# A hybrid decoder block on one core: every tile of its pool placed by hand

## The chip, the cores and the metric

The kernel runs on one core of one Trainium2 chip. The metric is device microseconds of one execution. Three runs of the kernel before took 1086.47, 1087.07 and 1087.11 us, so their median is 1087.07 us.

## The reference

One layer of a decoder, sequence 512, model width 1024, all in float32. It is cut here to what is computed.

```
h    = rms_norm(x)
proj = h @ w_in                    # glu | q | k | v | g | gate logits
a    = glu[..., :C] * sigmoid(glu[..., C:])
a    = silu(layer_norm(causal_depthwise_conv(a, 31 taps)))
y_a  = a @ w_conv_proj + b
r    = retention_chunkwise(rotary(q), rotary(k), v)   # 4 heads, dk 256, dv 512
y_b  = (silu(g) * head_norm(r)) @ w_ret_proj
x    = x + (sigmoid(gA) * y_a + sigmoid(gB) * y_b) @ w_out
u    = causal_depthwise_conv(rms_norm(x) @ w_up, 3 taps)
x    = x + (silu(u[..., :F]) * u[..., F:]) @ w_down   # F = 3072
out  = rms_norm(x)
```

## The kernel before

Activations are held transposed: 128 channels on the partitions, the 512 tokens along the row, so an activation tile is 128 x 512 in float32, 2048 bytes in each partition. Every activation that a matmul reads is split in two tiles of type float32r, a high and a low part, by ACT (a cast, L170 or L177) and DVE (a subtraction, L171 or L178). Weights come as one stream of 184 pieces of 128 x 1024 (4096 bytes in each partition, 8 blocks of 128 x 128): `load_half` (L93) loads a piece into `wraw`, `split_half` (L100) makes `whi` and `wlo` of it, again with ACT (L106) and DVE (L107). Each of the three tags has three buffers, and a piece is asked for two pieces ahead (`LOOK`).

Nearly all matmuls stand in `unit` (L143). For every block of weights there are three, each with 512 columns: the weight block is the stationary operand, which an own instruction (LDWEIGHTS) loads, the activation tile is the moving one.

```
wh, wl = blocks(1)
nc.tensor.matmul(ps, lhsT=wh, rhs=xh, start=kt == 0, stop=False)   # L147
nc.tensor.matmul(ps, lhsT=wh, rhs=xl, start=False, stop=False)     # L148
nc.tensor.matmul(ps, lhsT=wl, rhs=xh, start=False, stop=kt == last) # L149
```

Which tag the moving tile has depends on the stage:

- Four heads, one after the other: the gated convolution's, q's, k's and g's units move `xg` (the input). `values` (L421) is the other way round: `xg` is stationary and `whi` or `wlo` moves (L426 to L428). `ret_proj` of the head before moves `R`. `scores` (L452) has `A` on both sides, with 512, 384, 256 and 128 columns (L458 to L462); `inner` (L472) moves `sh` and `sl` against stationary `A` (L483 to L485).
- Gates and the last head's projection move `xg` and `R` in turns. The convolution's projection moves `A` (high) and `C` (low). The output projection moves `xg` (the mix).
- The up-projection moves `A`. The down-projection runs in two halves, the first over `xg` and `R`, the second over `C` and `xg`; its last two units are cut into halves of 256 tokens (L635 to L637).
- Sums over channels and their spread (L238, L191, L222) are a few dozen matmuls with `onesr`, `ones` and `identr`.

All tiles come from one pool, `sb`. A tag's buffers are laid out one behind another when the tag's first tile is asked for, so the order in which the program first asks for tags sets every address. Before, that order is the order of first use: `par` (2112 bytes) comes first, then `ones`, `neghalf` and so on as the code needs them. The same code lines set the order of the work: the scheduler orders instructions by the place where they are written and by `tc.high_priority`.

```
def t512(tag, bufs, dt=F32):                                        # L69
    return sb.tile([P, S], dt, tag=tag, bufs=bufs, name=nm(tag))
raw = sb.tile([P, HS], F32, tag="wraw", bufs=3, name=nm("wraw"))    # L94, whi and wlo alike
```

Of the kernel before, what the change touches and what calls it, by code (L numbers as in the profile page):

```python
# [9 lines left out]
F32 = mybir.dt.float32  # L10
F32R = mybir.dt.float32r
# [3 lines left out]
P = 128  # L15
S = 512
D = 1024
KT = D // P
# [3 lines left out]
NCH = S // P  # L22
# [3 lines left out]
FK = 3  # L26
EPS = 1e-6
HS = 8 * P
LOOK = 2
WARM = 9  # L30
WPRIO = 100
# [16 lines left out]
def hybrid_block(  # L48
# [11 lines left out]
    sb = ctx.enter_context(tc.tile_pool(name="sb", bufs=1))  # L60
# [4 lines left out]
    def nm(s):  # L65
        uid[0] += 1
        return f"{s}_{uid[0]}"

    def t512(tag, bufs, dt=F32):  # L69
        return sb.tile([P, S], dt, tag=tag, bufs=bufs, name=nm(tag))  # L70

    def tmp():
        return t512("t", 8)

    def bank():
        return psp.tile([P, S], F32, tag="ps", name=nm("ps"))

    def f32(ap):
        return ap.bitcast(F32)

    par = sb.tile([P, NPARAM], F32, tag="par", name="par")

    def pcol(name, i):
        c = _PC[name] + i
        return par[:, c:c + 1]
# [5 lines left out]
    raws = {}  # L91

    def load_half(h):  # L93
        raw = sb.tile([P, HS], F32, tag="wraw", bufs=3, name=nm("wraw"))  # L94
        cut = (0, 2 * P, HS) if h == 0 else (0, HS)
        raws[h] = raw, [slice(u, v) for u, v in zip(cut, cut[1:])]
        for sl in raws[h][1]:
            nc.sync.dma_start(out=raw[:, sl], in_=wst[h][:, sl])

    def split_half(h):  # L100
        raw, sls = raws.pop(h)
        hi = sb.tile([P, HS], F32R, tag="whi", bufs=3, name=nm("whi"))
        lo = sb.tile([P, HS], F32R, tag="wlo", bufs=3, name=nm("wlo"))
        with tc.high_priority(offset=WPRIO if h > 1 else 0):
            for sl in sls:
                nc.scalar.copy(out=hi[:, sl], in_=raw[:, sl])  # L106
                nc.vector.tensor_tensor(out=lo[:, sl], in0=raw[:, sl], in1=f32(hi[:, sl]),  # L107
                                        op=ALU.subtract)
        halves[h] = (hi, lo)

    def upto(h):
        while emitted[0] <= min(h, NBLK - 1):
            load_half(emitted[0])
            split_half(emitted[0])
            emitted[0] += 1
# [3 lines left out]
    def blocks(n):  # L119
        b = pos[0]  # L120
        pos[0] += n
        h, c = divmod(b, 8)
        upto(h + LOOK)
        hi, lo = halves[h]
# [18 lines left out]
    def unit(ps, rhs):  # L143
        last = len(rhs) - 1
        for kt, (xh, xl) in enumerate(rhs):
# [4 lines that stand above are left out]
        tick()  # L150
        return ps
# [15 lines left out]
    def split(src, tag, bufs):  # L167
        h = t512(tag, bufs, F32R)
        l = t512(tag, bufs, F32R)
        nc.scalar.copy(out=h, in_=src)  # L170
        nc.vector.tensor_tensor(out=l, in0=src, in1=f32(h), op=ALU.subtract)  # L171
        return h, l
# [21 lines left out]
    def tok(dt=F32):  # L194
        if dt == F32R:
            return sb.tile([P, NCH], F32R, tag="tokr", bufs=4, name=nm("tokr"))
        return sb.tile([P, NCH], F32, tag="tok", bufs=8, name=nm("tok"))
# [73 lines left out]
        later(wait[0], second)  # L271


    ones = sb.tile([P, P], F32, tag="ones", name="ones")
    nc.gpsimd.memset(ones, 1.0)
    neghalf = sb.tile([P, NCH], F32, tag="neghalf", name="neghalf")
    nc.gpsimd.memset(neghalf, -0.5)
    warm = tok()
    nc.scalar.copy(out=warm, in_=neghalf)
    warm_ps = bank()  # L280
    for _ in range(WARM):
        nc.tensor.matmul(warm_ps[:, 0:P], lhsT=ones, rhs=ones, start=True, stop=True)
    xs = []
    g0 = sb.tile([P, KT], F32, tag="g0", name="g0")
    for i in range(KT):
        t = t512("x", 8)
        nc.sync.dma_start(out=t, in_=xT[i * P:(i + 1) * P, :])
        xs.append(t)
        if i == 0:
            nc.sync.dma_start(out=g0, in_=params[:, _PC["norm_mix_g"]:_PC["norm_mix_g"] + KT])  # L290
            load_half(0)
        if i == 3:
            load_half(1)
    ident = sb.tile([P, P], F32, tag="ident", name="ident")
    nc.sync.dma_start(out=ident, in_=ident_in)
    nc.sync.dma_start(out=par, in_=params)
    identr = sb.tile([P, P], F32R, tag="identr", name="identr")
    nc.gpsimd.tensor_copy(out=identr, in_=ident)
    onesr = sb.tile([P, P], F32R, tag="onesr", name="onesr")
    nc.gpsimd.tensor_copy(out=onesr, in_=ones)  # L300
    xg = []
    for i in range(KT):
        xg.append(split_scaled(xs[i], g0[:, i:i + 1], "xg", 16))
        if i in (0, 3):
            split_half(emitted[0])
            emitted[0] += 1
# [13 lines left out]
    ss = SumSq()  # L320
    with tc.high_priority(offset=-200):
        for i in range(KT):
            ss.add(xs[i])
    r_tok = sb.tile([P, 4 * NCH], F32, tag="rtok", name="rtok")[:, 0:NCH]
    rB = [None]
    cosr = sb.tile([P, S], F32, tag="cosr", name="cosr")
    sinr = sb.tile([P, S], F32, tag="sinr", name="sinr")

    def norm_mix(b, ps):
        rB[0] = b  # L330
# [6 lines left out]
    def times_r(ps):  # L337
        t = tmp()
        nc.vector.tensor_tensor(out=t, in0=ps, in1=rB[0], op=ALU.mult)  # L339
        return t  # L340
# [106 lines left out]
    SOFF = (0, 512, 896, 1152)  # L447

    def scores(q, k, dec):
        sh = sb.tile([P, 1280], F32R, tag="sh", name=nm("sh"))  # L450
        sl_ = sb.tile([P, 1280], F32R, tag="sl", name=nm("sl"))
        for j in range(NCH):  # L452
            n = S - j * P
            ps = bank()
            js = slice(j * P, (j + 1) * P)
            for d in range(2):
                (qh, ql), (kh, kl) = q[d], k[d]
                nc.tensor.matmul(ps[:, :n], lhsT=kh[:, js], rhs=qh[:, j * P:], start=d == 0,  # L458
                                 stop=False)
                nc.tensor.matmul(ps[:, :n], lhsT=kh[:, js], rhs=ql[:, j * P:], start=False,  # L460
                                 stop=False)
                nc.tensor.matmul(ps[:, :n], lhsT=kl[:, js], rhs=qh[:, j * P:], start=False,  # L462
                                 stop=d == 1)
            t = tmp()
            nc.vector.tensor_tensor(out=t[:, :n], in0=ps[:, :n], in1=dec[:, :n], op=ALU.mult)
            o = slice(SOFF[j], SOFF[j] + n)
            nc.scalar.copy(out=sh[:, o], in_=t[:, :n])
            nc.vector.tensor_tensor(out=sl_[:, o], in0=t[:, :n], in1=f32(sh[:, o]),
                                    op=ALU.subtract)
        return sh, sl_  # L470
# [48 lines left out]
    for h in range(H):  # L519
        ps = [glu_units() for _ in range(2)] if h else glu_first()  # L520
        for i in range(2):
            a = glu(*ps[i])
            with tc.high_priority(offset=-1200):
                conv(2 * h + i, a)
        dec = t512("dec", 1)
        nc.sync.dma_start(out=dec, in_=decay[h])
        q = rope()
        k = rope()
        if rg is not None:
            ret_proj(h - 1, rg)  # L530
        v = values()
        sc = scores(q, k, dec)
        sgs = []
        for e in range(DV // P):
            t = times_r(unit(bank(), xg))
            s_ = t512("G", 4)
            nc.scalar.activation(out=s_, in_=t, func=AF.Silu)
            sgs.append(s_)
        banks = inner(sc, v)
        rg = ret_norm(h, banks, sgs)  # L540
# [16 lines left out]
    for m in range(KT):  # L557
        ps = unit(bank(), cv)
        t = tmp()
# [4 lines left out]
    ss = SumSq()  # L564
# [31 lines left out]
    def up_units():  # L596
        return unit(bank(), x1g), unit(bank(), x1g)
# [12 lines left out]
    first = [up_units() for _ in range(2)]  # L610
# [6 lines left out]
    ss = SumSq()  # L617
# [81 lines left out]
def _weight_stream(w_in, w_conv_proj, w_ret_proj, w_out, w_up, w_down):  # L699
# [14 lines left out]
    def rp(h):  # L714
        w = w_ret_proj[h * DV:(h + 1) * DV].reshape(4, P, KT // 2, 2, P)
        return w.transpose(2, 1, 3, 0, 4).reshape(KT // 2, P, HS)

    for h in range(H):
        for i in (2 * h, 2 * h + 1):
            pair = np.stack((wi[i], wi[KT + i]))  # L720
            if i == 0:
                pair = pair.reshape(2, P, KT, P).transpose(1, 2, 0, 3).reshape(P, 2, HS)
                pair = pair.transpose(1, 0, 2)
# [68 lines left out]
```

## Time and profile before

| | |
|---|---|
| median of three runs | 1087.07 us |
| the profiled execution | 1086.47 us |
| its span, first to last instruction | 1084.7 us |
| PE busy | 1073.2 us (99%) |
| PEld (weight loads, beside the matmuls) busy | 883.2 us (81%) |
| DVE busy | 770.0 us (71%) |
| ACT busy | 418.3 us (39%) |
| mean DMA rate over the span | 99 GB/s |

A busy time is the union of an engine's instructions. A matmul's row is longer than the distance to the next matmul, because the next one starts before the last one's results are out; so what one matmul costs in a stream is read from the starts of its rows, not from their durations. Line numbers here and in the rows are those of the kernel before.

### The profile page before, as it was taken

To read this page: it belongs to the slowest core of one execution; us is meant where nothing else is said; L and a number is where in the kernel's file an instruction comes from. 1 tells how busy PE (TensorE), PEld (TensorE's weight loads), DVE (VectorE), ACT (ScalarE), POOL (GpSimd) and SP (SyncE) were. 2 spreads that over 40 slices of the span, in tenths; PEclk is the share of its full clock that TensorE was granted. 3 is DMA by queue.
4 is the path that set the end of the run, shared out by engine and by line. 5 is a ranking of instruction groups with operands and counts; after the bars stand their busy time and mean duration, and the time that the engine had idled before them with its cause. 6 is when DMAs were issued, how large, how long until landed. Compare 5 with 4: busy or idle time off the path is not lost.

```text
span 1084.7 us, 12428 instructions
## 1 busy us (share of the span) xinstructions
PE 1073.2 (99%) x4834; PEld 883.2 (81%) x4834; DVE 770.0 (71%) x1126; ACT 418.3 (39%) x556; POOL 24.8 (2%) x88
## 2 busy tenths in 40 slices
PE   8999999999999999999999999999999999999996
PEld 6888888888888888888888888888888888888886
DVE  7899899758996699948764555677676236767433
ACT  6334332533234331535542234444443113444331
POOL 1000000000000000000000000000000000000000
PEclk9999999999999999999999999999999999999999
DMA  7223232323322232222323532332222223222212
GB/s 274 91 98 105 68 99 95 107 68 98 98 97 88 72 110 99 81 78 88 107 98 107 146 117 98 88 113 85 94 97 97 97 98 98 90 86 97 98 58 79
DMA packets 33259, 107.33 MB, mean 99 GB/s; under 512 B 3952, under 2 KB 6256, under 8 KB 33200
## 3 DMA queue, kind: packets, MB, share of 16 engines
q1 hardware_dynamic: 32416, 104.69, 29.1%
q0 software_dynamic: 784, 1.85, 1.0%
q8 instruction: 38, 0.62, 0.2%
q14 instruction: 21, 0.17, 0.1%
HBM read 104.41 MB, written 2.11 MB: 98 GB/s over the span
## 4 chain that ended last, share of the span: by engine, by line
PE 97%; issue 1%; DVE 1%; DMA 0%; SPq 0%; POOLq 0%; ACT 0%; POOL 0%; DVEq 0%
PE ps L147 28%; PE ps L149 28%; PE ps L148 28%; PE ps L427 3%; PE ps L426 3%; PE ps L428 3%; PE ps L484 1%; PE ps L485 1%; PE ps L483 1%; PE ps L460 0%; PE ps L462 0%; PE ps L458 0%; DVE ss L183 0%; DMA x<-in_xT_dram 0%; PE ps L238 0%
## 5 line engine op out<-in xcount | busy, mean ns | idle before, releaser
L106 ACT CAST whi<-wraw 128x1024 fp32r<-128x1024 f32 (+1 forms) x185 | 193.2, 1045 | 356.5 <-PE ps L148 258.3
L107 DVE TENSOR_TENSOR wlo<-wraw,whi 128x1024 fp32r<-128x1024 f32 (+1 forms) x185 | 224.7, 1215 | 62.1 <-ACT whi L106 61.9
L147 PE MATMUL ps<-xg,whi 128*128 128x512 f32 x672 | 262.1, 390 | 0.0
L148 PE MATMUL ps<-xg,whi 128*128 128x512 f32 x672 | 261.7, 389 | 0.0
L149 PE MATMUL ps<-xg,wlo 128*128 128x512 f32 x672 | 261.5, 389 | 0.0
L149 PE MATMUL ps<-A,wlo 128*128 128x512 f32 x448 | 176.5, 394 | 0.0
L147 PE MATMUL ps<-A,whi 128*128 128x512 f32 x448 | 176.5, 394 | 0.0
L368 DVE SCALAR_TENSOR_TENSOR C<-ap,par,C 128x512 f32<-128x512 f32 x240 | 166.4, 744 | 2.9 <-ACT C L365 2.6
L148 PE MATMUL ps<-A,whi 128*128 128x512 f32 x384 | 151.3, 394 | 0.0
L149 PEld LDWEIGHTS ps<-xg,wlo 128*128 128x128 f32 x672 | 126.2, 188 | 26.5
L147 PEld LDWEIGHTS ps<-xg,whi 128*128 128x128 f32 x672 | 126.2, 188 | 26.1
L148 PEld LDWEIGHTS ps<-xg,whi 128*128 128x128 f32 x672 | 126.2, 188 | 26.1
L149 PEld LDWEIGHTS ps<-A,wlo 128*128 128x128 f32 x448 | 83.8, 187 | 20.9
L147 PEld LDWEIGHTS ps<-A,whi 128*128 128x128 f32 x448 | 83.8, 187 | 20.7
L148 PEld LDWEIGHTS ps<-A,whi 128*128 128x128 f32 x384 | 71.8, 187 | 17.7
L589 DVE SCALAR_TENSOR_TENSOR t<-ap,par,t 128x512 f32<-128x512 f32 x96 | 71.7, 750 | 2.3 <-ACT t L586 0.7
L339 DVE TENSOR_TENSOR t<-ps,rB 128x512 f32<-128x512 f32 x48 | 32.5, 685 | 55.2 <-PE ps L149 55.2
L183 DVE TENSOR_TENSOR x<-x,ps 128x512 f32<-128x512 f32 (+1 forms) x50 | 33.0, 663 | 53.4 <-PE ps L149 49.9
L583 DVE TENSOR_TENSOR ap<-ps,rB 128x512 f32<-128x512 f32 x48 | 33.1, 691 | 48.4 <-PE ps L149 45.5
L147 PE MATMUL ps<-R,whi 128*128 128x512 f32 x160 | 63.0, 394 | 0.0
L148 PE MATMUL ps<-R,whi 128*128 128x512 f32 x160 | 63.0, 394 | 0.0
L149 PE MATMUL ps<-R,wlo 128*128 128x512 f32 x160 | 63.0, 394 | 0.0
(147 smaller groups left out, 1175.8 us busy)
## 6 DMA issues: line engine op xcount, KB each, us to landing
wraw<-in_wst_dram SPq DMA_DIRECT2D x183, 512.0 KB, 3.3
x<-in_xT_dram SPq DMA_DIRECT2D x16, 256.0 KB, 2.7
out_dram<-t SPq DMA_DIRECT2D x8, 256.0 KB, 2.3
nB<-row POOLq DMA_DIRECT2D x5, 256.0 KB, 4.7
dec<-in_decay_dram SPq DMA_DIRECT2D x4, 256.0 KB, 2.6
t<-in_cs_dram SPq DMA_DIRECT2D x2, 256.0 KB, 4.0
rB<-row POOLq DMA_DIRECT2D x2, 256.0 KB, 4.1
wraw<-in_wst_dram SPq DMA_DIRECT2D x1, 384.0 KB, 3.7
```

Source lines behind the costliest of these rows:

```text
L106: nc.scalar.copy(out=hi[:, sl], in_=raw[:, sl])
L107: nc.vector.tensor_tensor(out=lo[:, sl], in0=raw[:, sl], in1=f32(hi[:, sl]), op=ALU.subtract)
L147: nc.tensor.matmul(ps, lhsT=wh, rhs=xh, start=kt == 0, stop=False)
L148: nc.tensor.matmul(ps, lhsT=wh, rhs=xl, start=False, stop=False)
L149: nc.tensor.matmul(ps, lhsT=wl, rhs=xh, start=False, stop=kt == last)
L183: nc.vector.tensor_tensor(out=acc, in0=acc, in1=v, op=ALU.add)
L368: nc.vector.scalar_tensor_tensor(out=acc, in0=a[:, k:k + S], scalar=wcol(k), in1=acc, op0=ALU.mult, op1=ALU.add)
L426: nc.tensor.matmul(banks[c], lhsT=xh[:, sl], rhs=wh, start=kt == 0, stop=False)
L427: nc.tensor.matmul(banks[c], lhsT=xl[:, sl], rhs=wh, start=False, stop=False)
L428: nc.tensor.matmul(banks[c], lhsT=xh[:, sl], rhs=wl, start=False, stop=kt == KT - 1)
L583: nc.vector.tensor_tensor(out=u[:, FK - 1:], in0=ps, in1=rB[0], op=ALU.mult)
L589: nc.vector.scalar_tensor_tensor(out=c, in0=u[:, k:k + S], scalar=wcol(k), in1=c, op0=ALU.mult, op1=ALU.add)
```

## The change

No operation is added or taken away. All tiles of the pool but `junk`, `ap`, `vs`, `vm` and `tokr` are asked for at the top of the function, in an order written by hand; `first` keeps the first tile of each tag until the old place asks for it, through `t512` or the new helper `wide`. Small tiles stand first, then all tiles of 2048 bytes, then the weights' and the scores', and `par` behind them. The built programs hold the same instructions on every engine in the same order, with the same waits.

```
+    first = {}
     def t512(tag, bufs, dt=F32):
+        if tag in first:
+            t = first.pop(tag)
+            assert t.dtype == dt, tag
+            return t
         return sb.tile([P, S], dt, tag=tag, bufs=bufs, name=nm(tag))
...
+    ones = sb.tile([P, P], F32, tag="ones", name="ones")
+    ident = sb.tile([P, P], F32, tag="ident", name="ident")
+    identr = sb.tile([P, P], F32R, tag="identr", name="identr")
+    neghalf = sb.tile([P, NCH], F32, tag="neghalf", name="neghalf")
+    g0 = sb.tile([P, KT], F32, tag="g0", name="g0")
+    r_tok = sb.tile([P, 4 * NCH], F32, tag="rtok", name="rtok")[:, 0:NCH]
+    warm = sb.tile([P, NCH], F32, tag="tok", bufs=8, name="warm")
+    for tag, bufs, dt in (("x", 8, F32), ("xg", 16, F32R), ("A", 16, F32R), ("C", 8, F32),
+                          ("R", 8, F32R), ("G", 4, F32), ("ss", 2, F32), ("t", 8, F32),
+                          ("rB", 1, F32), ("nB", 1, F32), ("dec", 1, F32)):
+        first[tag] = sb.tile([P, S], dt, tag=tag, bufs=bufs, name=nm(tag))
+    cosr = sb.tile([P, S], F32, tag="cosr", name="cosr")
+    sinr = sb.tile([P, S], F32, tag="sinr", name="sinr")
+    for tag, dt in (("wraw", F32), ("whi", F32R), ("wlo", F32R)):
+        first[tag] = sb.tile([P, HS], dt, tag=tag, bufs=3, name=nm(tag))
+    for tag in ("sh", "sl"):
+        first[tag] = sb.tile([P, SW], F32R, tag=tag, name=nm(tag))
+    onesr = sb.tile([P, P], F32R, tag="onesr", name="onesr")
     par = sb.tile([P, NPARAM], F32, tag="par", name="par")
+
+    def wide(tag, dt, n, bufs):
+        if tag in first:
+            return first.pop(tag)
+        return sb.tile([P, n], dt, tag=tag, bufs=bufs, name=nm(tag))
...
-        raw = sb.tile([P, HS], F32, tag="wraw", bufs=3, name=nm("wraw"))
+        raw = wide("wraw", F32, HS, 3)
...
-        hi = sb.tile([P, HS], F32R, tag="whi", bufs=3, name=nm("whi"))
-        lo = sb.tile([P, HS], F32R, tag="wlo", bufs=3, name=nm("wlo"))
+        hi = wide("whi", F32R, HS, 3)
+        lo = wide("wlo", F32R, HS, 3)
...
-        sh = sb.tile([P, 1280], F32R, tag="sh", name=nm("sh"))
-        sl_ = sb.tile([P, 1280], F32R, tag="sl", name=nm("sl"))
+        sh = wide("sh", F32R, SW, 1)
+        sl_ = wide("sl", F32R, SW, 1)
```

The addresses that follow from the two orders, in bytes within a partition. "Over 512" and "over 2048" are the remainders of the first buffer's address; the buffers of a tag lie 2048 or 4096 bytes apart, so all of them have the same two.

| tag (buffers x bytes) | before | over 512 | over 2048 | after | over 512 | over 2048 |
|---|---|---|---|---|---|---|
| par (1 x 2112) | 16512 | 128 | 128 | 219648 | 0 | 512 |
| ones (1 x 512) | 18624 | 192 | 192 | 16512 | 128 | 128 |
| identr (1 x 512) | 48640 | 0 | 1536 | 17536 | 128 | 1152 |
| onesr (1 x 512) | 49152 | 0 | 0 | 219136 | 0 | 0 |
| x (8 x 2048) | 19456 | 0 | 1024 | 18432 | 0 | 0 |
| wraw (3 x 4096) | 35840 | 0 | 1024 | 172032 | 0 | 0 |
| xg (16 x 2048) | 49664 | 0 | 512 | 34816 | 0 | 0 |
| whi (3 x 4096) | 82432 | 0 | 512 | 184320 | 0 | 0 |
| wlo (3 x 4096) | 94720 | 0 | 512 | 196608 | 0 | 0 |
| t (8 x 2048) | 111104 | 0 | 512 | 145408 | 0 | 0 |
| C (8 x 2048) | 140736 | 448 | 1472 | 100352 | 0 | 0 |
| A (16 x 2048) | 159168 | 448 | 1472 | 67584 | 0 | 0 |
| sh (1 x 5120) | 192192 | 192 | 1728 | 208896 | 0 | 0 |
| sl (1 x 5120) | 197312 | 192 | 704 | 214016 | 0 | 1024 |
| R (8 x 2048) | 212672 | 192 | 1728 | 116736 | 0 | 0 |

## Rows read from the trace of the kernel before

**Rows 1.** The page: span, engines' busy time, chain that ended last.
```profile
span 1084.7 us, 12428 instructions
...
PE 1073.2 (99%) x4834; PEld 883.2 (81%) x4834; DVE 770.0 (71%) x1126; ACT 418.3 (39%) x556; POOL 24.8 (2%) x88
...
PE 97%; issue 1%; DVE 1%; DMA 0%; SPq 0%; POOLq 0%; ACT 0%; POOL 0%; DVEq 0%
```

**Rows 2.** Waits of PE, longest of 7: us in total, times, longest.
```profile
PE ps L222 <- DVE tokr L215: 1.2, 1, 1.2
```

**Rows 3.** Groups by line and form: xcount | busy us, mean ns.
```profile
L147 PE MATMUL ps<-xg,whi 128*128 128x512 f32 x672 | 262.1, 390 | 0.0
...
L147 PE MATMUL ps<-A,whi 128*128 128x512 f32 x448 | 176.5, 394 | 0.0
...
L148 PE MATMUL ps<-A,whi 128*128 128x512 f32 x384 | 151.3, 394 | 0.0
...
L147 PE MATMUL ps<-R,whi 128*128 128x512 f32 x160 | 63.0, 394 | 0.0
...
L148 PE MATMUL ps<-C,whi 128*128 128x512 f32 x88 | 34.7, 394 | 0.0
...
L147 PE MATMUL ps<-C,whi 128*128 128x512 f32 x24 | 9.5, 394 | 0.0
```

**Rows 4.** Timeline of PE, `xg` moving, first and last of 143: start us, us.
```profile
118.72 0.39 PE L147 MATMUL ps<-xg,whi 128*128 128x512 f32 x1
...
150.91 0.39 PE L148 MATMUL ps<-xg,whi 128*128 128x512 f32 x1
```

**Rows 5.** Timeline of PE: 96 rows of `values`, six of `scores` at 512 columns.
```profile
52.30 0.39 PE L426 MATMUL ps<-whi,xg 128*128 128x512 f32 x1
...
74.06 0.39 PE L458 MATMUL ps<-A,A 128*128 128x512 f32 x1
...
75.43 0.33 PE L458 MATMUL ps<-A,A 128*128 128x384 f32 x1
```

**Rows 6.** Timeline of PE: 96 rows of `R` in `ret_proj`, then `values`.
```profile
151.36 0.39 PE L147 MATMUL ps<-R,whi 128*128 128x512 f32 x1
...
173.76 0.39 PE L426 MATMUL ps<-whi,xg 128*128 128x512 f32 x1
...
174.91 0.39 PE L428 MATMUL ps<-wlo,xg 128*128 128x512 f32 x1
```

**Rows 7.** Timeline of PE, `A` moving in the up-projection: first, last of 169.
```profile
895.76 0.39 PE L147 MATMUL ps<-A,whi 128*128 128x512 f32 x1
...
934.96 0.39 PE L147 MATMUL ps<-A,whi 128*128 128x512 f32 x1
```

**Rows 8.** Timeline of PE at 256 columns: 12 rows of `C`, 24 of `xg`.
```profile
1055.92 0.28 PE L635 MATMUL ps<-C,whi 128*128 128x256 f32 x1
...
1057.33 0.28 PE L635 MATMUL ps<-xg,whi 128*128 128x256 f32 x1
...
1060.20 0.29 PE L635 MATMUL ps<-C,whi 128*128 128x256 f32 x1
```

**Rows 9.** Timeline of PE, first pass of `inner`: nine rows apart.
```profile
99.68 0.39 PE L483 MATMUL ps<-sh,A 128*128 128x512 f32 x1
...
101.27 0.22 PE L483 MATMUL ps<-sh,A 128*128 128x128 f32 x1
```

**Rows 10.** Groups by line and form, on DVE.
```profile
L171 DVE TENSOR_TENSOR xg<-t,xg 128x512 fp32r<-128x512 f32 x24 | 16.5, 688 | 10.3 <-ACT xg L170 10.3
...
L171 DVE TENSOR_TENSOR R<-G,R 128x512 fp32r<-128x512 f32 x16 | 10.9, 684 | 0.0
```

**Rows 11.** Three stretches: busy us of PE, PEld, DVE, ACT, POOL; clock, DMA.
```profile
151.00:174.00 23.00, 23.00 (x101) 18.44 (x100) 23.00 (x34) 9.21 (x14) 0.00 (x0) 1.00 0.31 99
440.00:528.00 88.00, 88.00 (x411) 74.06 (x410) 59.97 (x102) 40.60 (x59) 4.57 (x8) 1.00 0.28 88
894.00:1006.00 112.00, 112.00 (x482) 89.76 (x481) 77.01 (x96) 46.52 (x58) 1.72 (x17) 1.00 0.29 94
```

More of the change, by code (lines that the diff above doesn't have):

```diff
@@ L28 @@
 HS = 8 * P
+SW = 1280
 LOOK = 2
@@ L271, in stat @@
         later(wait[0], second)
-    ones = sb.tile([P, P], F32, tag="ones", name="ones")
     nc.gpsimd.memset(ones, 1.0)
-    neghalf = sb.tile([P, NCH], F32, tag="neghalf", name="neghalf")
     nc.gpsimd.memset(neghalf, -0.5)
-    warm = tok()
     nc.scalar.copy(out=warm, in_=neghalf)
@@ L283, in hybrid_block @@
     xs = []
-    g0 = sb.tile([P, KT], F32, tag="g0", name="g0")
     for i in range(KT):
@@ L293, in hybrid_block @@
             load_half(1)
-    ident = sb.tile([P, P], F32, tag="ident", name="ident")
     nc.sync.dma_start(out=ident, in_=ident_in)
     nc.sync.dma_start(out=par, in_=params)
-    identr = sb.tile([P, P], F32R, tag="identr", name="identr")
     nc.gpsimd.tensor_copy(out=identr, in_=ident)
-    onesr = sb.tile([P, P], F32R, tag="onesr", name="onesr")
     nc.gpsimd.tensor_copy(out=onesr, in_=ones)
@@ L323, in hybrid_block @@
             ss.add(xs[i])
-    r_tok = sb.tile([P, 4 * NCH], F32, tag="rtok", name="rtok")[:, 0:NCH]
     rB = [None]
-    cosr = sb.tile([P, S], F32, tag="cosr", name="cosr")
-    sinr = sb.tile([P, S], F32, tag="sinr", name="sinr")
     def norm_mix(b, ps):
```

## The prediction

> **What bounds the kernel now.** I read the page first: PE is busy for 1073.2 of 1084.7 us and holds 97% of the chain that ended last [rows 1]. Then the waits: the longest wait of PE for another engine is 1.2 us [rows 2], so between start and tail nothing but the matmul stream itself sets the time. The only question is how far apart two matmuls start, and whether that distance depends on an address.
>
> The groups by line give a first hint: matmuls of one shape last 390 ns with `xg` moving and 394 ns with `A`, `R` or `C` [rows 3]. Those durations overlap, so I took the distance of starts from the timeline:
>
> - `xg` moving: (150.91 - 118.72) / 142 = 226.7 ns [rows 4].
> - `whi` and `wlo` moving, `xg` stationary: (74.06 - 52.30) / 96 = 226.7 ns [rows 5].
> - `R` moving: (173.76 - 151.36) / 96 = 233.3 ns [rows 6].
> - `A` moving: (934.96 - 895.76) / 168 = 233.3 ns [rows 7].
>
> All have 512 columns, stationary blocks of the same size and the granted clock at 1.00, 2.4 GHz [rows 11]. `R` stands between stretches of `xg` and of `values`, with the same DVE load and DMA traffic around it, so the stage is not the cause. What the three tags at 233.3 share in the table of addresses: they start at a remainder of 448 or 192 over 512 bytes. What the others share: they start at a multiple of 512 (none at a multiple of 2048; all have 512 over 2048).
>
> **The change, part by part.** No instruction, wait or queue entry is added, removed or reordered, and no tile gets more or fewer buffers. So the sum has only terms of duration.
>
> 1. *Full-width matmuls that move `A`, `R` or `C`.* `A`: 448 + 384 + 448, where the third line's count equals the first's; `R`: 3 x 160; `C`: 24 + 88 + 24 [rows 3]. Together 1896. After the change these tiles have the same remainder over 512 as `xg`, and the same distance to `whi` and `wlo` over 512. I give them the distance of `xg`: 1896 x (233.3 - 226.7) = 1896 x 6.65 ns = 12.6 us less, all of it on the path, because PE waits for nobody there. Their ends: 0 if the remainder is not the cause, 12.6 us if it is.
> 2. *`xg`, `whi` and `wlo` moving.* They go from 512 to 0 over 2048. I take 0. The row for that: with 256 columns `xg` runs 1024 bytes from 512 to 1536 over 2048 and crosses no multiple of 2048, at (1060.20 - 1057.33) / 24 = 119.6 ns [rows 8]. At 2.4 GHz 256 columns are 106.7 ns and 512 are 213.3 ns, so the excess is 12.9 ns without a crossing, and 226.7 - 213.3 = 13.4 ns with one. A crossing costs nothing that shows.
> 3. *`scores` and `inner`.* All their operands were off 512 and all come to multiples of it. Six 512-column matmuls of `scores` take 1.37 us, 228 ns each [rows 5], so at 226.7 they gain 0.01 us a head. A pass of `inner` takes 1.59 us for three matmuls each of 512, 384 and 256 columns [rows 9]; at the columns' rate of `xg`, 3456 x 226.7 / 512 = 1.53 us, so at most 0.06 us a pass, 16 passes, 1.0 us. The other end comes from rows 8: at 256 columns `C` takes (1057.33 - 1055.92) / 12 = 117.5 ns and `xg` 119.6, so a multiple of 512 can also cost 2.1 ns; 288 matmuls in both places, 0.6 us. I take 0.3 us less, nearer to the full-width rows.
> 4. *The last two units.* 2 units x 2 halves x 4 tiles x 3 = 48 matmuls of 256 columns move `C` and go from 117.5 to 119.6 ns: 0.1 us more.
> 5. *The first matmuls behind a stretch at 233.3.* The five intervals from the end of `R` take 1.15 us, 230 ns each instead of 226.7 [rows 6], 17 ns that go with that stretch; such places stand 3 times after `ret_proj`, 3 in the gates, twice around the up-projection's start and middle and 13 times in the down-projection, 21 in all: 0.3 us less.
> 6. *Other engines.* The same subtraction takes 688 ns on `xg` and 684 ns on `R` [rows 10], so DVE sees no address. I take 0 for DVE, ACT, the DMAs and `par`, `identr` and `ones`, which move to other remainders but feed a few dozen short matmuls.
>
> What is late next: a faster PE asks for weights every 24 x 226.7 ns = 5.44 us instead of 5.60. Stretches with `xg` run at that pace already without a wait. In the stretch of `R`, DVE is busy all of the 23 us, but with convolution that may run late; three such stretches bring PE forward by 3 x 96 x 6.65 ns = 1.9 us in all, and in 440 to 528 us DVE is idle for 28 of 88 us. With `A` in the up-projection it is busy 77 of 112 us [rows 11]. So nothing is given back.
>
> The sum: -12.6 - 0.3 + 0.1 - 0.3 = -13.1 us. The profiled execution took 1086.47 us, 1.8 us beyond its span and 0.6 below the median of the three runs; it becomes 1073.4 us, and the median 1074.0 us.
>
> A rule that would widen this: the Trainium skill, page "TensorE: Matmul & The Clock Gate", section "Back-to-back issue gap", gives 518 cycles for a 512-column matmul at the full clock, 215.8 ns. The trace disagrees: its best stretch is at 226.7 ns. If hand placement brought the page's gap to the 4296 full-width matmuls of units and `values`, the time would be some 47 us below 1074; I give this no share of the sum.
>
> **The rivals.**
>
> *A. A multiple of 2048 counts too.* 512 over 2048 has never been tried against 0 with 512 columns, and a second step of 6.65 ns may lie there. It would act on 672 x 3 + 4 x 96 + 1896 = 4296 matmuls: 28.6 us more, 1045.4 us. Against it speaks term 2. Chance 0.09.
>
> *B. The upper part of the memory is slow, not the remainder.* `A`, `C` and `R` lie above 131072 before, the other movers below. After, `A`, `C` and seven of eight tiles of `R` are below and gain, `whi` and `wlo` are above, and `values` loses: (1896 - 60 - 384) x 6.65 ns = 9.7 us, about 1077.4 us. Against it: in `scores` both operands lie above and take 228 ns. Chance 0.06.
>
> *C. Slower: it is the distance between moving tile and weights.* Before, weights lie below 131072, as does `xg`; `A`, `R` and `C` lie above. Suppose a matmul is slow if its two operands lie on different sides. After, weights are above and `xg`, `A`, `C` and most of `R` below: 2016 + 48 matmuls with `xg` and 384 of `values` pay 6.65 ns each, 16.3 us, and the old ones stay at 233.3: 1103 us. It decides as soon as `xg` rows stand 233 ns apart. For it: `scores`, with both operands above, is nearly fast [rows 5]. Against it: with 256 columns `C`, on the other side, is the faster one [rows 8]. Chance 0.05.
>
> *D. No change.* Addresses don't matter and 233.3 has another cause. The rows leave little room: `R` switches on and off with the tile's name alone [rows 6]. Then the time stays at 1087. Chance 0.06. A rule on this side is in the Trainium skill, page "SBUF — State Buffer", section "Who interferes with whom": TensorE's reads have ports of their own and wait for no one. It doesn't speak of start addresses; taken at its word it leaves no place for a read that is slower by where it starts, and would give this rival's time. Rows 4 and 6 speak against that reading.
>
> **How the numbers follow.** The forecast has the remaining 0.74. Its own range is 1074.0 with -1.3 and +1.5 for terms 3 to 5 and the spread of the runs (0.6 us). The range of 8 in 10 must take in one rival, and B is the nearest: 1071.5 to 1078.5 holds 0.80. One measurement of this kernel tells 0.2%, 2.2 us, from no change. Faster: forecast, A and B, 0.89. Same: D, 0.06. Slower: C, 0.05.
>
> **What would show it right or wrong.** In the profile after, stretches of `A`, `R` and `C` must stand 226.7 ns apart, with mean durations of 389 or 390 instead of 394 ns, and their rows must look like those of `xg` throughout. `xg` and `values` must stay at 226.7. Span, about 1071.6 us; PE still 99%, with no wait over 1.5 us between 25 and 1050 us. Rows of `xg` below 224 ns would mean A, rows of `values` at 233 with `xg` at 226.7 would mean B, `xg` at 233 C, and `A` still at 233 with `xg` unchanged D. If all rows are as forecast and the span isn't, a wait that I don't see has opened: I would look at L107 and at the waits of PE.

## The result, and the profile after

The changed kernel takes 1073.85 us (median of four runs, 1073.60 to 1074.95) against 1087.09 for the kernel before in the same comparison: a ratio of 0.988 with a 95% interval of 0.9863 to 0.9897. The forecast was 1074.0. The profiled execution took 1073.63 us. Lines are those of the changed kernel from here on: L147 to L149 became L178 to L180, L426 to L428 became L447 to L449.

The page: the span is 12.9 us shorter, and PE is still busy for 99% of it and holds 96% of the chain [rows 1].

```profile
span 1071.8 us, 12428 instructions
...
PE 1059.9 (99%) x4834; PEld 884.8 (83%) x4834; DVE 769.4 (72%) x1126; ACT 420.1 (39%) x556; POOL 25.3 (2%) x88
...
PE 96%; issue 1%; DVE 1%; DMA 0%; SPq 0%; POOLq 0%; ACT 0%; POOL 0%; DVEq 0%
```

The longest wait of PE is the same one, at the tail [rows 2].

```profile
PE ps L253 <- DVE tokr L246: 1.2, 1, 1.2
```

Groups by line and form (xcount | busy us, mean ns): the matmuls that move `A`, `R` and `C` now have the durations of `xg` [rows 3], and DVE's subtraction takes what it took [rows 10].

```profile
L178 PE MATMUL ps<-xg,whi 128*128 128x512 f32 x672 | 261.9, 390 | 0.0
...
L178 PE MATMUL ps<-A,whi 128*128 128x512 f32 x448 | 174.3, 389 | 0.0
...
L178 PE MATMUL ps<-R,whi 128*128 128x512 f32 x160 | 62.2, 389 | 0.0
...
L179 PE MATMUL ps<-C,whi 128*128 128x512 f32 x88 | 34.2, 389 | 0.0
...
L202 DVE TENSOR_TENSOR xg<-t,xg 128x512 fp32r<-128x512 f32 x24 | 16.6, 690 | 10.3 <-ACT xg L201 10.3
...
L202 DVE TENSOR_TENSOR R<-G,R 128x512 fp32r<-128x512 f32 x16 | 10.9, 683 | 0.0
```

The timeline of PE gives the distances of starts. `A` in the up-projection: (922.90 - 885.05) / 167 = 226.6 ns, 233.3 before [rows 7].

```profile
885.05 0.39 PE L178 MATMUL ps<-A,whi 128*128 128x512 f32 x1
...
922.90 0.39 PE L180 MATMUL ps<-A,wlo 128*128 128x512 f32 x1
```

`R` in `ret_proj`, then `values`: (173.29 - 151.53) / 96 = 226.7 ns, 233.3 before, and the five intervals behind it take 1.13 instead of 1.15 us [rows 6].

```profile
151.53 0.39 PE L178 MATMUL ps<-R,whi 128*128 128x512 f32 x1
...
173.29 0.39 PE L447 MATMUL ps<-whi,xg 128*128 128x512 f32 x1
...
174.42 0.39 PE L449 MATMUL ps<-wlo,xg 128*128 128x512 f32 x1
```

`xg`: (150.85 - 118.89) / 141 = 226.7 ns, as before [rows 4], though it went from 512 to 0 over 2048.

```profile
118.89 0.39 PE L178 MATMUL ps<-xg,whi 128*128 128x512 f32 x1
...
150.85 0.39 PE L178 MATMUL ps<-xg,whi 128*128 128x512 f32 x1
```

At 256 columns `C` comes to (1044.24 - 1042.81) / 12 = 119 ns and `xg` to (1047.12 - 1044.24) / 24 = 120 [rows 8].

```profile
1042.81 0.28 PE L656 MATMUL ps<-C,whi 128*128 128x256 f32 x1
...
1044.24 0.28 PE L656 MATMUL ps<-xg,whi 128*128 128x256 f32 x1
...
1047.12 0.28 PE L656 MATMUL ps<-C,whi 128*128 128x256 f32 x1
```

The first pass of `inner` comes from 1.59 [rows 9] to 1.57 us. Its three matmuls of 512 columns take 100.56 - 99.88 = 0.68 us; those of the second pass, which follows on matmuls of 128 columns, take 102.48 - 101.73 = 0.75 us.

```profile
99.88 0.39 PE L504 MATMUL ps<-sh,A 128*128 128x512 f32 x1
...
100.56 0.33 PE L504 MATMUL ps<-sh,A 128*128 128x384 f32 x1
...
101.45 0.22 PE L504 MATMUL ps<-sh,A 128*128 128x128 f32 x1
...
101.73 0.44 PE L504 MATMUL ps<-sh,A 128*128 128x512 f32 x1
...
102.48 0.33 PE L504 MATMUL ps<-sh,A 128*128 128x384 f32 x1
```

The second pass before, 0.74 us for the same three:

```profile
101.55 0.44 PE L483 MATMUL ps<-sh,A 128*128 128x512 f32 x1
...
102.29 0.33 PE L483 MATMUL ps<-sh,A 128*128 128x384 f32 x1
```

I also added up, from all rows of both traces, the distances from each matmul to the next by what they move. The 1896 of term 1 give 12.63 us, `xg` and `values` 0.6, `scores` and `inner` together 0.1, and the 256-column ones of `C` take back 0.16.

### The profile page after: what moved, and what is told of

Same layout as the page of the kernel before. It is cut to its first block, busy times and chain, and to the rows that moved or that the text cites. A ratio compares the mean times of both kernels' runs of the same rounds, so it can differ in the third digit from the quotient of the medians.

```text
span 1071.8 us, 12428 instructions
## 1 busy us (share of the span) xinstructions
PE 1059.9 (99%) x4834; PEld 884.8 (83%) x4834; DVE 769.4 (72%) x1126; ACT 420.1 (39%) x556; POOL 25.3 (2%) x88
## 4 chain that ended last, share of the span: by engine, by line
PE 96%; issue 1%; DVE 1%; DMA 0%; SPq 0%; POOLq 0%; ACT 0%; POOL 0%; DVEq 0%
PE ps L179 28%; PE ps L178 28%; PE ps L180 28%; PE ps L449 3%; PE ps L447 3%; PE ps L448 3%; PE ps L505 1%; PE ps L506 1%; PE ps L504 1%; PE ps L481 0%; PE ps L483 0%; PE ps L479 0%; DVE ss L214 0%; DMA x<-in_xT_dram 0%; PE ps L269 0%
## 5 line engine op out<-in xcount | busy, mean ns | idle before, releaser
L178 PE MATMUL ps<-xg,whi 128*128 128x512 f32 x672 | 261.9, 390 | 0.0
L180 PE MATMUL ps<-xg,wlo 128*128 128x512 f32 x672 | 261.4, 389 | 0.0
L178 PE MATMUL ps<-A,whi 128*128 128x512 f32 x448 | 174.3, 389 | 0.0
L180 PE MATMUL ps<-A,wlo 128*128 128x512 f32 x448 | 174.3, 389 | 0.0
L179 PE MATMUL ps<-A,whi 128*128 128x512 f32 x384 | 149.4, 389 | 0.0
L180 PEld LDWEIGHTS ps<-xg,wlo 128*128 128x128 f32 x672 | 126.2, 188 | 26.1
L178 PEld LDWEIGHTS ps<-xg,whi 128*128 128x128 f32 x672 | 126.2, 188 | 25.9
L178 PEld LDWEIGHTS ps<-A,whi 128*128 128x128 f32 x448 | 84.1, 188 | 17.6
L180 PEld LDWEIGHTS ps<-A,wlo 128*128 128x128 f32 x448 | 84.1, 188 | 17.3
L178 PE MATMUL ps<-R,whi 128*128 128x512 f32 x160 | 62.2, 389 | 0.0
L180 PE MATMUL ps<-R,wlo 128*128 128x512 f32 x160 | 62.2, 389 | 0.0
```

## Experiments

The sum was right, but the forecast left two readings open. In the changed kernel every moving tile starts at a multiple of 512 (theory T), and every moving tile also lies a multiple of 512 from the weights (theory Q). Q, T and a theory of the place in the memory (U, which joins rivals B and C: the upper part, or the other side than the weights, costs time) were set against each other first.

**e1: only A, C and R off.** All else stays aligned, and the three lie lowest.

```
+    for tag, bufs, dt in (("A", 16, F32R), ("C", 8, F32), ("R", 8, F32R)):
+        first[tag] = sb.tile([P, S], dt, tag=tag, bufs=bufs, name=nm(tag))
     ones = sb.tile([P, P], F32, tag="ones", name="ones")
...
-    for tag, bufs, dt in (("x", 8, F32), ("xg", 16, F32R), ("A", 16, F32R), ("C", 8, F32),
-                          ("R", 8, F32R), ("G", 4, F32), ("ss", 2, F32), ("t", 8, F32),
-                          ("rB", 1, F32), ("nB", 1, F32), ("dec", 1, F32)):
+    for tag, bufs, dt in (("x", 8, F32), ("xg", 16, F32R), ("G", 4, F32), ("ss", 2, F32),
+                          ("t", 8, F32), ("rB", 1, F32), ("nB", 1, F32), ("dec", 1, F32)):
```

> The changed kernel with A, C and R asked for first, so that they start at a remainder of 128 over 512 and lie lowest of all; every other tile that TensorE reads keeps a multiple of 512, the weights stay above 131072. Theory T (a full-width matmul costs 6.65 ns more when its moving tile starts off a multiple of 512): A, C and R at 233.3 ns, xg at 226.7; 1896 x 6.65 ns = 12.6 us more than the changed kernel, 1086.5 us. Theory Q (what counts is the remainder between moving tile and weights over 512): the same 1086.5 us. Theory U (lying in the upper part of the memory, or on another side than the weights, is what cost time; the remainder does not): A, C and R lie low and stay at 226.7, 1073.9 us.

Measured: 1086.22 us, ratio to the kernel before 0.9992 (0.9983 to 1.0002). Timeline of PE, `A` in the up-projection, 159 intervals: 233.3 ns.

```profile
894.35 0.39 PE L179 MATMUL ps<-A,whi 128*128 128x512 f32 x1
...
931.44 0.40 PE L179 MATMUL ps<-A,whi 128*128 128x512 f32 x1
```

The whole gain is gone, with `A`, `C` and `R` low in the memory, while `xg` and `values` stay at 226.7 ns. U falls.

**e2: the kernel before, 64 bytes further.**

```
-    r_tok = sb.tile([P, 4 * NCH], F32, tag="rtok", name="rtok")[:, 0:NCH]
+    r_tok = sb.tile([P, 8 * NCH], F32, tag="rtok", name="rtok")[:, 0:NCH]
```

> The kernel before with one number changed: the tile rtok is 128 instead of 64 bytes, so that all tiles behind it move up by 64 bytes. C and A come to a multiple of 512 (they stay above 131072, weights below), R, sh and sl to a remainder of 256. Theory T: A and C at 226.7 ns, 1416 x 6.65 ns = 9.4 us less; R stays at 233.3 if only 512 counts, 1077.7 us, and goes to 226.7 if a multiple of 256 is enough, 1074.5 us. Theory Q: the same. Theory U: nothing moves to the other side, A, C and R stay at 233.3, 1087.1 us.

Measured: 1074.47 us, ratio 0.9887 (0.987 to 0.9903). Timeline of PE: `A` stands 226.6 ns apart over 164 intervals, and `R`, at 256 over 512, 226.6 over 92.

```profile
885.73 0.39 PE L147 MATMUL ps<-A,whi 128*128 128x512 f32 x1
...
922.90 0.39 PE L149 MATMUL ps<-A,wlo 128*128 128x512 f32 x1
```

```profile
152.21 0.39 PE L147 MATMUL ps<-R,whi 128*128 128x512 f32 x1
...
173.06 0.39 PE L149 MATMUL ps<-R,wlo 128*128 128x512 f32 x1
```

One number does what the whole placement does, within what the two intervals can tell. `R` needs only a multiple of 256; it is the one long stretch in which a distance of 256 over 512 was tried, so that the distance counts over 256, and not over 512, rests on it.

**e3: everything off together.** The small tiles (`ones` to `warm`) move behind `sh` and `sl`:

```
-    ones = sb.tile([P, P], F32, tag="ones", name="ones")
...
     for tag in ("sh", "sl"):
         first[tag] = sb.tile([P, SW], F32R, tag=tag, name=nm(tag))
+    ones = sb.tile([P, P], F32, tag="ones", name="ones")
...
```

> The changed kernel with its small tiles asked for last instead of first, so that all tiles that TensorE reads (but onesr) start at a remainder of 128 over 512, moving tiles and weights alike. Theory T: every full-width matmul is at 233.3 ns; 4296 x 6.65 ns = 28.6 us more than the changed kernel and some 0.3 us for the 48 of the first pair, 1102.7 us. Theory Q: moving tile and weights are still a multiple of 512 apart, all stay at 226.7, 1073.9 us. Theory U: 1073.9 us.

Measured: 1074.62 us in one run. Timeline of PE, `xg` (139 intervals, 226.8 ns) and `A` (164, 226.6 ns), both starting at 128 over 512:

```profile
119.47 0.39 PE L178 MATMUL ps<-xg,whi 128*128 128x512 f32 x1
...
151.00 0.39 PE L179 MATMUL ps<-xg,whi 128*128 128x512 f32 x1
```

```profile
886.14 0.39 PE L178 MATMUL ps<-A,whi 128*128 128x512 f32 x1
...
923.31 0.39 PE L180 MATMUL ps<-A,wlo 128*128 128x512 f32 x1
```

Theory T, the reading that the forecast put first, falls: every moving tile is off a multiple of 512, and no long stretch stands above 227 ns.

**e4: only the weights off.**

```
+    for tag in ("whi", "wlo"):
+        first[tag] = sb.tile([P, HS], F32R, tag=tag, bufs=3, name=nm(tag))
     ones = sb.tile([P, P], F32, tag="ones", name="ones")
...
-    for tag, dt in (("wraw", F32), ("whi", F32R), ("wlo", F32R)):
-        first[tag] = sb.tile([P, HS], dt, tag=tag, bufs=3, name=nm(tag))
+    first["wraw"] = sb.tile([P, HS], F32, tag="wraw", bufs=3, name=nm("wraw"))
```

> The changed kernel with whi and wlo asked for first: they alone start at a remainder of 128 over 512 and lie lowest; all activations stay at a multiple of 512. Theory T: only values, where whi and wlo move, gets slower: 384 x 6.65 ns = 2.6 us, 1076.4 us; the stationary operand's start costs nothing. Theory Q: in every unit and in values the two operands are off each other, 4296 x 6.65 ns = 28.6 us, 1102.4 us. A third, S (the weight load itself costs time from an odd start): all units slower than 226.7 and values, whose stationary operand is xg, as T says.

Measured: 1098.81 us in one run, 25.0 above the changed kernel, where Q expected 28.6; a matmul pays 5.7 ns here, not 6.65. Timeline of PE, `xg` (139 intervals, 232.4 ns) and `A` (160, 232.4 ns), with all activations at multiples of 512:

```profile
121.68 0.39 PE L179 MATMUL ps<-xg,whi 128*128 128x512 f32 x1
...
153.99 0.39 PE L180 MATMUL ps<-xg,whi 128*128 128x512 f32 x1
```

```profile
907.00 0.39 PE L179 MATMUL ps<-A,whi 128*128 128x512 f32 x1
...
944.19 0.39 PE L180 MATMUL ps<-A,whi 128*128 128x512 f32 x1
```

Q holds: what counts is where the moving tile starts relative to the weights. e3, with the weights' start just as odd, takes the third theory, S, away. The price stands in the rows of the matmuls alone: those of the weight loads last 188 ns each in e4 and in the changed kernel, while the matmuls' own go from 389 to 395 ns. A rule on this: the Trainium skill, page "SBUF — State Buffer", section "Who interferes with whom", gives TensorE two independent read ports, one for the moving operand and one for the weight load. If the two reads were independent, each odd start would have a price of its own: 12.4 us for the moving tiles `A`, `C` and `R` (e1), 25.0 for the weights (e4), and more than either for both at once. Both at once (e3) cost 0.8 us; here the measurement decides. That the two reads collide is the reading that suggests itself; no run shows the collision itself.

**e5 and e6: other distances.** The tiles are asked for in these orders, with small ones between them to set the remainders:

```
# e5
whi, wlo (128); rtok; R (192); neghalf; A, C (224); g0, warm, ones, ident, identr; xg (0) and the rest
# e6
A, C (128); rtok; R (192); neghalf; whi, wlo (224); g0, warm, ones, ident, identr; xg (0) and the rest
```

> The changed kernel with its tiles in another order: whi and wlo start at 128 over 512, R at 192, A and C at 224, xg at 0. Theory Q now reads: a full-width matmul costs more when moving tile and weights are not a multiple of 256 bytes apart. Relative to the weights, R lies 64 over 256, A and C 96, xg and values 128. Q with one price for all: every matmul of units and values at 232 to 233 ns, about 6 ns more, 4296 x 6 = 26 us, 1099.7 us. Theory G (the price grows with the distance from a multiple of 256, up to the 6 ns seen at 128): R at 229.7, A and C at 231.2, xg at 232.5; 2064 and 384 x 6 + 1416 x 4.5 + 480 x 3 = 22.5 us, 1096.4 us. Theory T (only the moving tile's own remainder): xg stays at 226.7 and the time is below 1090 us.

> The changed kernel with its tiles in another order: A and C start at 128 over 512, R at 192, whi and wlo at 224, xg at 0. Relative to the weights xg lies 32 over 256, A and C 160, R 224. Q with one price: all at 232 to 233.3 ns, 4296 x 6 to 6.65 = 26 to 29 us, 1100 to 1102.4 us. Theory G: 32 and 224 are both 32 away from a multiple of 256 and cost 1.5 ns, 160 costs 4.5: (2064 + 384 + 480) x 1.5 + 1416 x 4.5 = 10.8 us, 1084.7 us. Should a distance of 32 be cheaper than a multiple of 256, xg falls below 226.7 ns.

Measured: 1099.14 and 1103.68 us, one run each; Q with one price comes to 1099.7 and to 1102.4 at most. Timeline of PE in e5, `R` at a distance of 64: (176.96 - 155.91) / 92 = 228.8 ns.

```profile
155.91 0.39 PE L182 MATMUL ps<-R,whi 128*128 128x512 f32 x1
...
176.96 0.40 PE L184 MATMUL ps<-R,wlo 128*128 128x512 f32 x1
```

`A` in e5, at 96: (944.09 - 906.76) / 160 = 233.3 ns.

```profile
906.76 0.39 PE L182 MATMUL ps<-A,whi 128*128 128x512 f32 x1
...
944.09 0.40 PE L183 MATMUL ps<-A,whi 128*128 128x512 f32 x1
```

In e6, `xg` at 32, (155.40 - 122.73) / 140 = 233.4 ns; `R` at 224, (177.80 - 156.33) / 92 = 233.4; `A` at 160, (948.38 - 911.14) / 159 = 234.2:

```profile
122.73 0.40 PE L182 MATMUL ps<-xg,whi 128*128 128x512 f32 x1
...
155.40 0.40 PE L184 MATMUL ps<-xg,wlo 128*128 128x512 f32 x1
```

```profile
156.33 0.40 PE L182 MATMUL ps<-R,whi 128*128 128x512 f32 x1
...
177.80 0.39 PE L184 MATMUL ps<-R,wlo 128*128 128x512 f32 x1
```

```profile
911.14 0.39 PE L182 MATMUL ps<-A,whi 128*128 128x512 f32 x1
...
948.38 0.40 PE L182 MATMUL ps<-A,whi 128*128 128x512 f32 x1
```

Together, the distance of starts by how far the moving tile starts from the weights, over 256:

| distance, bytes over 256 | ns | run, tile |
|---|---|---|
| 0 | 226.6, 226.7 | changed kernel, `A`, `R`, `xg`; e2, `R` |
| 32 | 233.4 | e6, `xg` |
| 64 | 228.8 | e5, `R` |
| 96 | 233.3 | e5, `A` |
| 128 | 232.4, 233.3 | e4, `A`; e1, `A` |
| 160 | 234.2 | e6, `A` |
| 192 | 233.3 | before, `A`, `R` |
| 224 | 233.4 | e6, `R` |

So one price for nearly all; G, which wanted a distance of 32 to be cheap, falls, and 64 is an exception that nothing here explains. Differences of a nanosecond in this table need not come from the distance: in e4 `values`, all at 128, stands at 233.2 ns in the first head and at 232.3 in the other three.

**e7: only `wlo` off.** `wlo` is asked for first, then the small tiles, the activations, `wraw` and `whi`; otherwise the changed kernel.

> The changed kernel with wlo alone off: it starts at 128 over 512, whi and all activations at multiples of 512. In a unit the matmuls follow each other with weights whi, whi, wlo. Theory N (what disturbs a matmul is the weight load of the next one, which runs beside it): the second matmul of each three stands 232.5 ns before the third, the first and the third stay at 226.7; in values, where wlo moves against loads of xg, the third of three is slower. Theory O (it is the matmul's own weights): the third of each three is slower, the first two not. Either way one matmul of three pays: 1448 in units and 128 in values, x 6 ns = 9.5 us, 1083.3 us.

Measured: 1092.14 us in one run, 18.3 above the changed kernel where 9.5 was expected. Groups by line and form, the three steps of a unit (L182 and L183 with `whi`, L184 with `wlo`), and the timeline of `A`, 161 intervals of 231.1 ns:

```profile
L184 PE MATMUL ps<-A,wlo 128*128 128x512 f32 x448 | 177.9, 397 | 0.0
L182 PE MATMUL ps<-A,whi 128*128 128x512 f32 x448 | 174.3, 389 | 0.0
L183 PE MATMUL ps<-A,whi 128*128 128x512 f32 x384 | 152.1, 396 | 0.0
```

```profile
901.34 0.39 PE L182 MATMUL ps<-A,whi 128*128 128x512 f32 x1
...
938.54 0.40 PE L184 MATMUL ps<-A,wlo 128*128 128x512 f32 x1
```

Neither N nor O alone. The second of three (its own weights in place, the next ones off) lasts 396 ns and the third (its own off, the next in place) 397; only the first keeps the 389 ns of a stream in place. The distances from each row's start to the next, averaged over all rows of each line that move `A`, are 226.7, 232.5 and 234.1 ns; their mean is the 231.1 of the stretch. In `values` only the third of three pays, the one that moves `wlo`: 225.9, 226.7 and 234.1 ns.

The expected 9.5 us had counted `values` twice: there are 1448 groups of three in all, 1320 in units and 128 in `values`, so that one payer in each would have cost 8.7 us. With two payers in the units the sum is 1320 x (5.8 + 7.4) ns + 128 x 7.4 ns = 18.4 us, and 18.3 were measured.

**e8 and e9: R in steps of 32 bytes, and 16 between.** `R`'s tiles are 8 columns wider, so its eight buffers lie 2080 bytes apart; e9 reads each from 16 bytes further. `R` is asked for ahead of `xg`, and the sums that read `ident` take its copy `identr`.

```
+            n = S + 8 if tag == "R" else S
+            t = sb.tile([P, n], dt, tag=tag, bufs=bufs, name=nm(tag))
+        return t[:, 0:0 + S] if tag == "R" else t      # e9: t[:, 4:4 + S]
...
-    ident = sb.tile([P, P], F32, tag="ident", name="ident")
+    ident = tmp()[:, 0:P]
```

> The changed kernel with R's eight buffers 2080 instead of 2048 bytes apart (each tile 8 columns wider, the last 8 unused), everything else that TensorE reads at 256 over 512, so that the buffers of R lie 0, 32, 64 ... 224 over 256 relative to the weights: the whole curve in one run, read buffer by buffer. To make room, the identity's float32 copy is staged in a t tile. Theory Q with the prices so far: 0 at 226.7 ns, 64 at 229, 32, 96, 128, 160, 192 and 224 at 232.5 to 234.3; high tiles (0, 64, 128, 192; 320 matmuls) 3.8 ns dearer on average, low tiles (160 matmuls) 7 ns, 2.3 us more than the changed kernel, 1076.2 us. Theory T (own remainder over 512): all but the second buffers at 233, and all of xg, A and C too, since they start at 256 over 512: above 1095 us. Theory Q says of xg, A, C and values that they stay at 226.7.

> As the run before, but every tile of R is read from 16 bytes further: 16, 48, 80 ... 240 over 256. If a multiple of 256 is the best place there is, no buffer of R falls below 226.7 ns and all stand between that and 235, 1074 to 1077.5 us. If a start between two multiples of 32 is better than 0, a buffer falls below 226.7 ns, and a version that beats the changed kernel is to be had by putting every moving tile there.

Measured: 1082.40 and 1083.68 us, one run each, some 6 us above what was expected. Most of that is one wait of PE, 5.1 us in e8 and 5.3 in e9, where no other run has one over 1.2 (us in total, times, longest; e8). Staging the identity in a `t` tile is the likely reason; no run has it alone.

```profile
PE ps L274 <- ACT t L268: 5.1, 1, 5.1
```

Behind this wait the granted clock is 0.50, the lower of its two levels, 1.2 GHz, for a while: four matmuls in e8 and eleven in e9 start 427 ns apart, and cost some 0.9 and 2.3 us more than at the full clock. A stretch of e9 (busy us of PE, PEld, DVE, ACT, POOL; clock, DMA):

```profile
25.40:29.80 4.40, 4.40 (x12) 3.43 (x11) 2.63 (x18) 0.00 (x0) 2.19 (x3) 0.50 0.55 201
```

The distances answer half of the question. `R` in e8, first and last of 92 rows: (179.22 - 158.12) / 91 = 231.9 ns.

```profile
158.12 0.39 PE L183 MATMUL ps<-R,whi 128*128 128x512 f32 x1
...
179.22 0.39 PE L184 MATMUL ps<-R,whi 128*128 128x512 f32 x1
```

In sum `R` loses 480 x 5.1 ns = 2.4 us, near the 2.3 expected. Buffer by buffer the expectation failed. With the buffers counted in the order in which the program asks for them, the rows that move the one at distance 0 stand 230.2 ns before the next on average in e8, not 226.7, although that tile and all weights are in place. A matmul's distance therefore depends on its neighbours' places too, and a curve can't be read from a mixed stream: in e9 the rows of the buffer at 48 average 226.7 ns in the first `ret_proj` and 234.0 in the down-projection. Single rows say still less. They lie between 225 and 238 here, and between 227 and 241 in e4's long stretches of `xg`, where all have the same distance. All of `R` in e9 averages 230.4 ns, so this run shows no better place than 0, and can't rule one out. `xg`, `A`, `C` and `values`, all at 256 over 512 there like the weights, keep medians of 227 ns, as Q says.

## Why the prediction was right, and where its reason was not

- *PE's stream bounds, and nothing is given back.* Right: 99% busy, no new wait, and the time fell by what the stream lost.
- *Term 1.* The size is right: 12.6 us forecast, 12.63 measured, on exactly the tags named. The reason put ahead of it failed: "they start at a multiple of 512" is neither needed (e3, e2's `R`) nor enough (e4). What counts is the distance between moving tile and weights, over 256. The sum came out because the change aligns both at once, as the half-sentence on "the same distance to `whi` and `wlo`" had it; under either reading it is the same sum, so its coming out speaks for neither.
- *Term 2.* Right: in long stretches `xg` and `values` stay at 226.7 ns at a multiple of 2048; rival A falls.
- *Term 3.* Mis-sized: 0.3 us forecast, 0.1 measured. The term looked at each operand alone; in pairs, which is what counts, there was nothing to align: `sh` and `sl` at 192 and `A` at 448 over 512 were a multiple of 256 apart before too, and `scores` has `A` on both sides. All that was won stands in the first three rows of `scores` and of the first pass of `inner`, behind `xg` or `values`: 229, 233 and 231 ns before, 226 to 227 after. The later passes keep their 0.74 to 0.75 us for three, in place before and after. Nor is the columns' rate of `xg` the right yardstick for narrow matmuls: those of 384 columns in `inner` stand 170 to 178 ns apart in both kernels, where that rate gives 170.
- *Terms 4 and 5.* Right in sign, somewhat larger than forecast: 0.16 us back for `C` at 256 columns, where 0.1 was forecast, and 0.6 us won in `xg` and `values`. The 21 places of term 5 won 19 to 20 ns each, 0.41 us where 0.3 was forecast; the rest stands mostly in the first rows of `xg` behind `scores` and `inner`, which the forecast left out.
- *Term 6.* Right: 690 and 683 ns for the subtraction against 688 and 684.
- *Rival B* falls with the result, as `values` stays at 226.7 ns, and with e1: `A`, `C` and `R` lie low in the memory and stand 233.3 ns apart. *Rival C* falls with the result itself, yet its idea that the pair of operands counts was the right one; only the sides at 131072 were wrong. Its row in favour, `scores` at 228 ns with both operands at 448 over 512 [rows 5], was a pair a multiple of 512 apart.
- *Rival D* falls with e1 and e2.

## What to carry to other kernels

When TensorE is 99% busy, compare the distance of starts between stretches that differ only in the tile they move: here a matmul that moved `A` took 3% longer than one that moved `xg`, and nothing but the tile's name told their rows apart. Before asking for aligned addresses, ask what must be aligned to what; here the starts of moving tiles and weights have to lie a multiple of 256 bytes apart, and 64 bytes in one small tile were enough (e2). Small tiles and odd-sized ones belong at an end of the pool, or padded, so that they don't shift the tiles behind them.

## What the runs showed that was not expected

- The two operands of a 512-column matmul have a best distance among those tried: 226.7 ns at multiples of 256 bytes, 232 to 234 at six of seven other steps of 32, 228.8 at 64.
- At 256 columns the order is reversed, if by little: 117.5 ns off [rows 8], 119 to 120 in place.
- The price is not a matmul's own affair. e7's two of three, e8's mixed stream, the five intervals behind `R` before the change (230 ns, their own tiles in place) [rows 6], and the later passes of `inner`, where three matmuls in place take 0.75 us behind narrow ones, show that neighbours share it. Why 256, why 64 is cheaper, and what carries over from one matmul to the next stays open.
